# Sliding windows of an image batch: splitting every third store in the last loop, and copying on VectorE instead of ScalarE

## The chip, the core and the metric

The kernel runs on one core of a Trainium2 chip. The metric is the device time of one execution in microseconds. Before the change the median of three runs is 194.26 us (194.17 to 194.33).

## The reference: what is computed

The input `x` has 16 images of 64 channels, 64 x 64, in fp32. Every 8 x 8 window at a stride of 4 is copied out, so there are 15 x 15 windows and each element of the input goes to up to four of them. Nothing is calculated.

```python
batch, c, h, w = x.shape                 # 16, 64, 64, 64; window_size 8, stride 4
...
for i in range(n_h):                     # 15
    for j in range(n_w):                 # 15
        result[:, i, j] = x[:, :, 4*i : 4*i + 8, 4*j : 4*j + 8].copy()
```

The output is `[16, 15, 15, 64, 8, 8]`: 59 MB, from an input of 16.8 MB.

## The kernel before

**Layout.** A partition holds one image, one half of the channels (`CH` = 2, so 32 channels each) and one quarter of the rows (`HQ` = 4, so 16 rows each): 16 x 2 x 4 = 128 partitions. The whole input stays in SBUF as `L`, `[128, 32 channels, 16 rows, 64 columns]`. It is loaded in four chunks of channels with four DMAs each, issued in turn by SP and ACT; the first two chunks are the first half of a partition's channels.

**Windows.** The kernel works through 60 steps `(j, s)`: `j` is the column of the window (0 to 14) and `s` the place of its first row in a partition's quarter (0 to 3). One step makes, on all partitions at once, the windows of one column and of four rows of windows. `window(j, s, half)` gathers 32 channels x 8 x 8 elements per partition into the buffer `G`, and stores them from there with one indirect DMA, issued by POOL (GpSimd). A partition's piece of the output is one run of 8 KB; the row of the output that it goes to comes from an index tile. For `s` = 3 the window reaches into the next quarter: four rows are copied from the own partition (L103) and four are shuffled in from the next partition (L104), both on DVE (VectorE), and the last quarter of each image, which has no such window, is dropped by an index out of bounds. This is called a *last* window below (`idx_last`, `idx_hlast`). For `s` = 0, 1, 2 there is one copy (L101), on ACT (ScalarE).

**Wholes and halves.** With `half` = None a step is one *whole*: 32 channels, 2048 elements and 8 KB per partition, 1 MB in all (three quarters of it for a last window). With `half` = 0 or 1 it covers 16 of the channels: 1024 elements, 4 KB per partition. Halves use the output seen with rows of 4 KB (`o_h`, `idx_h`), wholes the one with rows of 8 KB (`o_v`, `idx`).

**Buffers.** `G` has 18 units, each for a half; a whole takes two. They are used in turn, so a copy waits until the store that last read its unit has finished. The stores are declared free of dependences among each other. Each uses one of eight semaphores, so a store waits for the eighth before it: at most eight are in flight.

**Order.** `order` goes over `j`, and within it over `s`. The first twelve steps store their first half early (L123), because only the first two chunks of the input must have landed for that. Then come six rounds of two second halves of those steps and two wholes of the following steps (L127). The last loop (L133) stores the remaining 36 steps, `j` from 6 to 14, as wholes. The framework schedules the instructions on each engine; in the trace POOL issues the first three last halves before the others, and otherwise follows the program.

Of the kernel before, what the change touches and what calls it, by code (L numbers as in the profile page):

```python
# [1 line left out]

# [4 lines left out]


@with_exitstack  # L10
def kernel(
    ctx: ExitStack,
    tc: tile.TileContext,
    x: bass.AP,
    window_size: int,
    stride: int,
    out: bass.AP,
):
    nc = tc.nc
    P = nc.NUM_PARTITIONS  # L20

    B, C, H, W = x.shape
    Bo, NH, NW, Co, WSo, WSo2 = out.shape
    WS = int(window_size)
    ST = int(stride)
    assert Bo == B and Co == C and WSo == WS and WSo2 == WS

    f32 = mybir.dt.float32
    i32 = mybir.dt.int32
    ALU = mybir.AluOpType  # L30
    HQ = 4
    CH = P // (B * HQ)
    CL = C // CH
    RB = H // HQ
    NSLOT = RB // ST
    NWIN = NH * NW
    CFREE = CL * WS * WS
    assert HQ == 4 and CH == 2 and WS == 2 * ST

    lpool = ctx.enter_context(tc.tile_pool(name="lpool", bufs=1))  # L40
    ipool = ctx.enter_context(tc.tile_pool(name="ipool", bufs=1))
    gpool = ctx.enter_context(tc.tile_pool(name="gpool", bufs=1))


    L = lpool.tile([P, CL, RB, W], f32)
    x_v = x.rearrange("b (ch cl) (hq r) w -> hq (b ch) cl (r w)", ch=CH, hq=HQ)
    NCH = 4
    cw = CL // NCH
    for k in range(NCH):
        for q in range(HQ):  # L50
            (nc.sync, nc.scalar)[q % 2].dma_start(
                out=L[q::HQ, k * cw : (k + 1) * cw, :, :],
                in_=x_v[q, :, k * cw : (k + 1) * cw, :],
            )


    def itile(name):
        return ipool.tile([P, 1], i32, name=name)

    pi, tb, tq, tc_, idx, idx_last = (itile(n) for n in ("pi", "tb", "tq", "tc", "idx", "idx_last"))  # L60
    nc.gpsimd.iota(pi[:, :], pattern=[[0, 1]], base=0, channel_multiplier=1)  # L61
    nc.vector.tensor_scalar(out=tb[:, :], in0=pi[:, :], scalar1=3, scalar2=None, op0=ALU.logical_shift_right)  # L62
    nc.vector.tensor_scalar(out=tc_[:, :], in0=pi[:, :], scalar1=2, scalar2=1, op0=ALU.logical_shift_right, op1=ALU.bitwise_and)  # L63
    nc.vector.tensor_scalar(out=tq[:, :], in0=pi[:, :], scalar1=HQ - 1, scalar2=None, op0=ALU.bitwise_and)  # L64
    nc.vector.tensor_scalar(out=tb[:, :], in0=tb[:, :], scalar1=float(NWIN * CH), scalar2=None, op0=ALU.mult)  # L65
    nc.vector.tensor_tensor(out=tb[:, :], in0=tb[:, :], in1=tc_[:, :], op=ALU.add)  # L66
    nc.vector.tensor_scalar(out=tc_[:, :], in0=tq[:, :], scalar1=float(NSLOT * NW * CH), scalar2=None, op0=ALU.mult)  # L67
    nc.vector.tensor_tensor(out=idx[:, :], in0=tb[:, :], in1=tc_[:, :], op=ALU.add)  # L68

    nc.vector.tensor_scalar(out=tq[:, :], in0=tq[:, :], scalar1=float(HQ - 1), scalar2=float(2 * B * NWIN * CH), op0=ALU.is_equal, op1=ALU.mult)  # L70
    nc.vector.tensor_tensor(out=idx_last[:, :], in0=idx[:, :], in1=tq[:, :], op=ALU.add)  # L71


    HCL = CL // 2
    idx_h, idx_hlast = itile("idx_h"), itile("idx_hlast")
    for d, e in ((idx_h, idx), (idx_hlast, idx_last)):
        nc.vector.tensor_scalar(out=d[:, :], in0=e[:, :], scalar1=2.0, scalar2=None, op0=ALU.mult)  # L77
    o_v = out.rearrange("b i j (ch cl) r w -> (b i j ch) (cl r w)", ch=CH)
    o_h = out.rearrange("b i j (ch cl) r w -> (b i j ch) (cl r w)", ch=2 * CH)
    nxt = [min(p + 1, 31) for p in range(32)]  # L80


    UNITS = 18
    G = gpool.tile([P, UNITS * HCL, WS, WS], f32, name="G")
    at = 0

    def window(j, s, half):
        nonlocal at
        cols = slice(j * ST, j * ST + WS)
        last = s == NSLOT - 1  # L90
        if half is None:
            n, c0 = 2, 0
            at += at % 2
        else:
            n, c0 = 1, half * HCL
        u = at % UNITS
        at += n
        cs = slice(c0, c0 + n * HCL)
        g = G[:, u * HCL : (u + n) * HCL, :, :]
        if not last:  # L100
            nc.scalar.copy(out=g, in_=L[:, cs, s * ST : s * ST + WS, cols])  # L101
        else:
            nc.vector.tensor_copy(out=g[:, :, 0:ST, :], in_=L[:, cs, s * ST : RB, cols])  # L103
            nc.vector.stream_shuffle(out=g[:, :, ST:WS, :], in_=L[:, cs, 0:ST, cols], mask=nxt)  # L104
        if half is None:
            o, ix = o_v, (idx_last if last else idx)
        else:
            o, ix = o_h, (idx_hlast if last else idx_h)
        st = nc.gpsimd.indirect_dma_start(  # L109
            out=o,  # L110
            out_offset=bass.IndirectOffsetOnAxis(ap=ix[:, 0:1], axis=0),
            in_=g.rearrange("p c r w -> p (c r w)"),
            in_offset=None,
            element_offset=(s * NW + j) * CH * CFREE + (half or 0) * HCL * WS * WS,
            bounds_check=B * NWIN * CH * (1 if half is None else 2) - 1,
            oob_is_err=False,
        )
        tc.declare_no_dep(st.ins, group="stores", reason="each store writes rows of its own")
        tc.add_to_no_dep_group("stores", st.ins)

    order = [(j, s) for j in range(NW) for s in range(NSLOT)]
    EARLY = 12
    for j, s in order[:EARLY]:  # L123
        window(j, s, 0)
    late = list(order[:EARLY])
    rest = list(order[EARLY:])
    while late:  # L127
        for w in late[:2]:
            window(*w, 1)
        for w in rest[:2]:  # L130
            window(*w, None)
        late, rest = late[2:], rest[2:]
    for w in rest:  # L133
        window(*w, None)


# [1 line left out]
_INS = ['x', 'window_size', 'stride']  # L138
_OUTS = [((16, 15, 15, 64, 8, 8), 'float32')]

_NUMBERS = {'window_size': 8, 'stride': 4}


# [26 lines left out]
```

## Time and profile before

| what | value |
|---|---|
| median of three runs | 194.26 us |
| the profiled execution: its time, and its span from first to last instruction | 194.17 us, 192.4 us |
| DVE, ACT, POOL busy | 30.4, 86.2, 70.3 us |
| HBM read, and stored by the POOL queue | 16.78 MB, 58.99 MB |
| stores: wholes, last wholes, halves, last halves | 36, 12, 18, 6 |
| one POOL issue of a store | 0.97 us |
| a whole copied on ACT; a half | 1.90 us; 1.04 us |
| half of a whole last window copied on DVE; shuffled | 0.69 us; 1.28 us |
| store, from issue to landing (whole; half) | 18.2 us; 13.6 us |
| last POOL issue; end of DMA traffic | 170.6 us; about 188.6 us |

Busy time is the time in which an engine executes; waiting and issuing of plain DMAs are not counted. "DMA share" is the mean busy share of the core's 16 DMA engines; it can come out slightly over 1, because consecutive packets overlap by a few ns. GB/s counts all that those engines moved, both ways.

### The profile page before, as it was taken

Reading aid. Unit: us, or ns where it says so; the run is one execution under the profiler, and the core shown is the slowest. Engines: PE = TensorE matmul, PEld = TensorE weight load, DVE = VectorE, ACT = ScalarE, POOL = GpSimd, SP = SyncE. Lnnn points to the kernel's source line nnn. Section 1 sums busy time; section 2 is a strip of 40 time slices with the busy share of each in tenths; the row PEclk is TensorE's granted clock in tenths of the full one; section 3 lists DMA queues with packets and bytes.
Section 4 is the critical chain, followed back from the end, with each engine's and each line's share of the span. In section 5 each row is a group of like instructions: output and inputs, shape, how many; then the busy total and the mean of one; then the engine's idle time right before and its main releaser. Section 6 shows DMA issues by size and latency. Waiting matters only on the chain.

```text
span 192.4 us, 478 instructions
## 1 busy us (share of the span) xinstructions
DVE 30.4 (16%) x65; ACT 86.2 (45%) x55; POOL 70.3 (37%) x77
## 2 busy tenths in 40 slices
DVE  2000050000232302303030122121121203030000
ACT  0000049500699875373747465646565655600000
POOL 0000027723367766456363253434343434440000
DMA  5999999999999999999999999999999999999960
GB/s 183 418 413 410 410 410 414 417 417 422 420 421 427 429 414 429 404 403 418 412 409 409 419 404 409 416 405 409 409 412 409 409 411 412 407 409 414 424 257 17
DMA packets 14724, 75.80 MB, mean 394 GB/s; under 512 B 1984, under 2 KB 1984, under 8 KB 8960
## 3 DMA queue, kind: packets, MB, share of 16 engines
q0 software_dynamic: 10368, 58.99, 75.3%
q1 hardware_dynamic: 2176, 8.39, 11.0%
q10 hardware_dynamic: 2176, 8.39, 10.8%
q14 instruction: 4, 0.03, 0.0%
HBM read 16.78 MB, written 62.91 MB: 414 GB/s over the span
## 4 chain that ended last, share of the span: by engine, by line
DMA 65%; issue 19%; ACT 3%; POOL 1%; POOLq 1%; PEldq 0%
DMA out_dram<-G,idx_last 38%; DMA out_dram<-G,idx 14%; DMA out_dram<-G,idx_h 8%; DMA out_dram<-G,idx_hlast 6%; ACT G L101 3%; POOL out_dram L109 1%; POOLq L165 1%; POOLq L109 0%; POOL pi L61 0%; PEldq L165 0%
## 5 line engine op out<-in xcount | busy, mean ns | idle before, releaser
L101 ACT COPY G<-L 128x2048 f32<-128x2048 f32 (+1 forms) x54 | 84.9, 1613 | 54.4 <-DMA out_dram<-G,idx 18.6
L109 POOL DMA_INDIRECT out_dram<-G,idx x36 | 34.8, 966 | 47.0 <-DMA out_dram<-G,idx 43.1
L103 DVE COPY G<-L 128x1024 f32<-128x1024 f32 (+1 forms) x18 | 11.1, 618 | 138.3 <-DMA out_dram<-G,idx 62.8
L109 POOL DMA_INDIRECT out_dram<-G,idx_h x18 | 17.4, 966 | 13.9 <-DMA out_dram<-G,idx_hlast 4.3
L104 DVE STREAM_SHUFFLE G<-L 128x1024 f32<-128x1024 f32 (+1 forms) x18 | 19.6, 1090 | 0.0
L109 POOL DMA_INDIRECT out_dram<-G,idx_hlast x6 | 5.9, 990 | 27.9 <-DVE G L104 26.4
L109 POOL DMA_INDIRECT out_dram<-G,idx_last x12 | 11.8, 986 | 11.7 <-DVE G L104 6.8
L101 ACT ACT_TABLE_LOAD x1 | 1.3, 1283 | 26.6 <-DMA L<-in_x_dram 26.6
L62 DVE TENSOR_SCALAR tb<-pi 128x1 int32<-128x1 int32 x1 | 0.2, 155 | 1.0 <-POOL pi L61 1.0
L61 POOL IOTA pi<- 128x1 int32 x1 | 0.1, 120 | 0.4 <-PEq L165 0.4
L104 DVE LOAD_MASK_SELECT G<-L x18 | 0.2, 14 | 0.0
L151 POOL MEMSET const-float32-0.0<- 128x1 f32 x1 | 0.1, 100 | 0.2 <-issue 0.2
L68 DVE CUSTOM_DVE_ANT_0 idx<-tb,tc 128x2 uint16<-128x2 uint16 x1 | 0.2, 160 | 0.0
L66 DVE CUSTOM_DVE_ANT_0 tb<-tb,tc 128x2 uint16<-128x2 uint16 x1 | 0.2, 159 | 0.0
L67 DVE TENSOR_SCALAR tc<-tq 128x1 int32<-128x1 int32 x1 | 0.2, 154 | 0.0
L77 DVE TENSOR_SCALAR idx_hlast<-idx_last 128x1 int32<-128x1 int32 x1 | 0.2, 154 | 0.0
L77 DVE TENSOR_SCALAR idx_h<-idx 128x1 int32<-128x1 int32 x1 | 0.2, 154 | 0.0
L71 DVE CUSTOM_DVE_ANT_0 idx_last<-idx,tq 128x2 uint16<-128x2 uint16 x1 | 0.2, 153 | 0.0
L65 DVE TENSOR_SCALAR tb<-tb 128x1 int32<-128x1 int32 x1 | 0.2, 152 | 0.0
L70 DVE TENSOR_SCALAR tq<-tq 128x1 int32<-128x1 int32 x1 | 0.1, 148 | 0.0
L64 DVE TENSOR_SCALAR tq<-pi 128x1 int32<-128x1 int32 x1 | 0.1, 145 | 0.0
L63 DVE TENSOR_SCALAR tc<-pi 128x1 int32<-128x1 int32 x1 | 0.1, 144 | 0.0
(3 smaller groups left out, 0.3 us busy)
## 6 DMA issues: line engine op xcount, KB each, us to landing
L<-in_x_dram ACTq DMA_DIRECT2D x8, 1024.0 KB, 21.1
L<-in_x_dram SPq DMA_DIRECT2D x8, 1024.0 KB, 19.8
out_dram<-G,idx POOLq DMA_INDIRECT x36, 18.2
out_dram<-G,idx_h POOLq DMA_INDIRECT x18, 13.6
out_dram<-G,idx_last POOLq DMA_INDIRECT x12, 18.3
out_dram<-G,idx_hlast POOLq DMA_INDIRECT x6, 13.1
```

Source lines behind the costliest of these rows:

```text
L62: nc.vector.tensor_scalar(out=tb[:, :], in0=pi[:, :], scalar1=3, scalar2=None, op0=ALU.logical_shift_right)
L65: nc.vector.tensor_scalar(out=tb[:, :], in0=tb[:, :], scalar1=float(NWIN * CH), scalar2=None, op0=ALU.mult)
L66: nc.vector.tensor_tensor(out=tb[:, :], in0=tb[:, :], in1=tc_[:, :], op=ALU.add)
L67: nc.vector.tensor_scalar(out=tc_[:, :], in0=tq[:, :], scalar1=float(NSLOT * NW * CH), scalar2=None, op0=ALU.mult)
L68: nc.vector.tensor_tensor(out=idx[:, :], in0=tb[:, :], in1=tc_[:, :], op=ALU.add)
L71: nc.vector.tensor_tensor(out=idx_last[:, :], in0=idx[:, :], in1=tq[:, :], op=ALU.add)
L77: nc.vector.tensor_scalar(out=d[:, :], in0=e[:, :], scalar1=2.0, scalar2=None, op0=ALU.mult)
L101: nc.scalar.copy(out=g, in_=L[:, cs, s * ST : s * ST + WS, cols])
L103: nc.vector.tensor_copy(out=g[:, :, 0:ST, :], in_=L[:, cs, s * ST : RB, cols])
L104: nc.vector.stream_shuffle(out=g[:, :, ST:WS, :], in_=L[:, cs, 0:ST, cols], mask=nxt)
L109: st = nc.gpsimd.indirect_dma_start(out=o, out_offset=bass.IndirectOffsetOnAxis(ap=ix[:, 0:1], axis=0), in_=g.rearrange("p c r w -> p (c r ...
L165: with _tile.TileContext(nc) as tc:
```

## The change

Two things are changed. The copy of a window with `s` = 0, 1, 2 is done by VectorE instead of ScalarE, in all stages, so that all gathering stands in one engine's queue and ScalarE only issues loads. And the last loop goes in groups of three steps: the first is stored as two halves, the next two as wholes. The 36 steps of this loop thus make 24 stores of halves and 24 of wholes instead of 36 of wholes, and the kernel has 84 stores instead of 72. The first two loops keep their order. Bytes, layouts, buffers and indices stay as they are.

```diff
         if not last:
-            nc.scalar.copy(out=g, in_=L[:, cs, s * ST : s * ST + WS, cols])
+            nc.vector.tensor_copy(out=g, in_=L[:, cs, s * ST : s * ST + WS, cols])
         else:
...
-    for w in rest:
-        window(*w, None)
+    while rest:
+        window(*rest[0], 0)
+        window(*rest[0], 1)
+        for w in rest[1:3]:
+            window(*w, None)
+        rest = rest[3:]
```

## The prediction

> **What bounds the kernel now.** I read the page first, then the busy time by stretch, the groups by shape, the timeline around the two engines that the change touches, and at last the trace's own records of DMA packets and of semaphore increments. The page says that the sixteen DMA engines are full from the second slice to the thirty-eighth, while no compute engine is above 45%:
>
> ```profile
> DVE 30.4 (16%) x65; ACT 86.2 (45%) x55; POOL 70.3 (37%) x77
> ...
> DMA  5999999999999999999999999999999999999960
> GB/s 183 418 413 410 410 410 414 417 417 422 420 421 427 429 414 429 404 403 418 412 409 409 419 404 409 416 405 409 409 412 409 409 411 412 407 409 414 424 257 17
> ```
>
> So the end is bytes over rate: 16.8 MB read and 59.0 MB stored. A copy, an issue or a wait counts only if it empties the DMA queues or changes the rate. The stretches (span us, their length, then DVE, ACT and POOL busy, clock, DMA share, GB/s) show three rates:
>
> ```profile
> 40.00:50.00 10.00, 0.20 (x1) 0.25 (x1) 2.90 (x3) 1.00 1.03 420
> 59.00:74.00 15.00, 2.95 (x6) 13.06 (x11) 10.03 (x11) 1.00 1.02 425
> 74.00:80.00 6.00, 1.83 (x4) 2.84 (x2) 2.90 (x3) 1.00 1.01 414
> 80.00:96.00 16.00, 3.27 (x6) 8.88 (x5) 8.43 (x9) 1.00 1.02 409
> 110.00:125.00 15.00, 3.72 (x6) 8.96 (x5) 6.47 (x7) 1.00 1.01 408
> 125.00:140.00 15.00, 3.21 (x6) 8.12 (x5) 5.85 (x7) 1.00 1.01 410
> 140.00:155.00 15.00, 2.50 (x4) 9.49 (x5) 6.03 (x7) 1.00 1.01 410
> 155.00:170.00 15.00, 3.79 (x6) 7.59 (x4) 5.80 (x6) 1.00 1.01 409
> 170.00:183.00 13.00, 0.00 (x0) 0.00 (x0) 0.97 (x1) 1.00 1.01 416
> 184.60:188.00 3.40, 0.00 (x0) 0.00 (x0) 0.00 (x0) 1.00 0.51 214
> ```
>
> Up to 97 us the engines move halves and wholes mixed (the last half is issued at 82.7 and lands about 14 us later), after that wholes alone. The tempting reading is "mixed runs at 425, wholes at 409, so mix throughout". The third and fourth lines speak against it: from 74 to 96 the stores are still the same mix, two halves and two wholes in turn, and the rate is already (6 x 414 + 16 x 409)/22 = 410.4. The packet records say the same. Until 73.5 us a 4 KB packet takes 159 ns and an 8 KB one 309 ns, nearly without exception; from 74 us on the means are about 164 and 321 for both sizes, mixed or not. Whatever slows packets by 4% begins inside the mixed stage.
>
> The last line is the second thing to see: for 3.4 us at the end half of the engines work alone. Each store makes sixteen semaphore increments, one as each engine finishes. The gap between the eighth and the ninth is 0.01 us until 77 us, then grows: 0.08 at 84, 0.82 at 94, 1.32 at 101 (0.73 us per 10 us), and from there more slowly, 1.49 at 106 to 3.48 at 179 (0.28 per 10 us). Eight engines run ahead, and the other eight set the end.
>
> **The change, part by part.** The last loop holds 36 windows (j from 6 to 14), 27 of 1.0486 MB and 9 of 0.7864 MB (a quarter of the rows of a last window is dropped): 35.4 MB, in 12 groups of three. The change splits the first window of each group.
>
> *Bytes and rate.* The bytes stay. Now this stage runs at 409.2 (mean of the four 15 us lines): 86.5 us. In the new mix the nearest row by time and state is 74 to 96, at 410.4, which already holds the cost of smaller packets and of more stores: 86.2 us, so **-0.3 us**. For the other ends: the full-speed mix at 425 gives 83.3, or -3.2; and from the packets alone, at full speed 16 packets of 4 KB at 155.3 ns start to start against 8 of 8 KB at 305.7, plus 6 ns for one more semaphore write, is +45 ns for each of 12 splits, or +0.5 us. I take -0.3 because that stretch has both the mix and the slow packets; I see nothing in the diff that removes what made them slow.
>
> *The gap between the engines.* If it grows by 0.73 per 10 us in a mix and 0.28 with wholes, 73 us (101 to 174) add up to 3.3 us of gap. A gap of s costs s x (1 - 214/409) = 0.48 s, since half the engines still work in it: 0 to +1.6 us. I take the middle, **+0.8**, since the steep stretch is also the one in which the gap arose, and may not keep its slope.
>
> *Twelve more stores on POOL.* An issue takes 0.97 us and 0.30 until the next: 1.27. A group of three windows takes the DMA 2.95 MB / 409 = 7.2 us; POOL then needs 4 x 1.27 = 5.1 in place of 3.8. Each store waits for the eighth before it, so eight are in flight: now eight wholes, then six window-equivalents, about 14 us of transfer. POOL's wait of 1.5 us or so at each store (44.6 us in all, for the eighth store back) shrinks, and this cover hides the rest: **0**. Without it each store would cost 1.27 us. The Trainium skill, page "DMA: Bandwidth & Descriptors", section "Anatomy of one DMA", gives a fixed cost of about 2.0 us per DMA, which would make an estimated 24 us of twelve stores if they ran one after another; here landings of queued halves follow each other every 1.23 us, so that rule does not price this case.
>
> *The copies from ACT to DVE.* Lines by shape:
>
> ```profile
> L101 ACT COPY G<-L 128x2048 f32<-128x2048 f32 x36 | 68.0, 1898 | 40.6 <-DMA out_dram<-G,idx 18.6 <-DMA out_dram<-G,idx_last 10.6 <-DVE G L104 8.0
> ...
> L104 DVE STREAM_SHUFFLE G<-L 128x1024 f32<-128x1024 f32 x12 | 15.3, 1279 | 0.0
> L103 DVE COPY G<-L 128x1024 f32<-128x1024 f32 x12 | 8.3, 694 | 81.1 <-DMA out_dram<-G,idx 62.8 <-DMA out_dram<-G,idx_h 10.2 <-ACT G L101 8.1
> ```
>
> DVE copies 512 elements in 0.42 us undisturbed and 1024 in 0.69; at 0.27 per 512 more, 2048 take an estimated 1.23 us (2.5 at worst, at the shuffle's pace). A group then costs DVE 1.6 us for the split window and 2.8 for two wholes with their share of last ones, 4.4 of 7.2 us (7.2 at the worst pace). Now all copies stand in one queue, so a copy that waits for its buffer holds up all later ones, and behind them POOL's stores. But the 18 half-buffers hold three groups, twelve stores, and eight are in flight: four stores, some 7 us, lie between a free buffer and its issue. Today it is one store, 2.5 us, against an ACT copy of 1.9. **0**.
>
> *The start.* The twelve first halves take DVE 9 x 0.69 + 3 x 1.13 = 9.6 us from 26.0 on, faster than POOL issues them (15 us), under loads that fill the DMA until 49.6. From 49.8 the second halves come 0.69 us apart instead of 1.04, with four or five stores still in flight. ACT's table load of 1.3 us goes, hidden. **0**.
>
> Sum: -0.3 + 0.8 = +0.5 us. The profiled run took 194.17 (span 192.39 and 1.78 around it), the median is 194.26: so 194.8.
>
> **The rivals.** *Faster: the slow packets vanish.* If they come from a relation between the engines' places in their stores that wholes on end keep up, and the new order breaks it, the last stage runs at 425 (-3.2 us), and with the gap gone a further 0.48 x 2.9 = -1.4: 191.1 without and 189.7 with the second. For it: 15 us at 425 in just this mix. Against: 22 us at 410 in the same mix. The 416 of 170 to 183, when no engine computes, says that quiet helps little.
>
> *Slower: DVE copies keep POOL from writing its descriptors.* The trace has one clear meeting:
>
> ```profile
> 60.65 0.43 DVE L103 COPY G<-L 128x512 f32<-128x512 f32 x1 [5.50 <-DMA out_dram<-G,idx_h]
> 60.70 1.21 POOL L109 DMA_INDIRECT out_dram<-G,idx_last  x1 [0.30 <-DMA out_dram<-G,idx_h]
> ```
>
> The issue took 1.21 instead of 0.97 under 0.38 us of copy; at 74.60 a copy of 512 took 0.69 behind a running issue instead of 0.43. So they exclude each other in part, and the copies on DVE, 18 now, would be 84. At +0.24 per store a POOL group is 4 x 1.51 = 6.0 us, below 7.2. At full exclusion it is 5.1 plus 3.4 of copying, 8.5. The last-loop issues begin at 88.4; 12 x 8.5 and 3 us for the last transfer end at 193.4 instead of 188.6, which is +4.8: 199. It decides from (188.6 - 3 - 88.4)/12 = 8.1 us per group, since the last issue is now at 170.5 and may slip. The Trainium skill, page "SBUF — State Buffer", section on the two sides of SBUF, states that an fp32 copy on DVE within SBUF locks GpSimd out for the whole instruction, so that descriptors starve: taken whole, that is the 199. The measured 0.24 says that the lock costs less than the overlap, and eight queued stores cover it.
>
> *No change in order or effect.* The program's order need not be the loop's (three last halves go out first today); the same bytes in another order, at the same 409 and the same gap, give 194.3.
>
> **How the numbers follow.** Forecast, rate about 410 with a gap that grows by anything from nothing to the full slope (193.9 to 196.0): 0.53, its lower part being "no change". Slow packets gone, wholly or partly (189.7 to 193.8): 0.34. POOL or DVE bound (above 196, up to 199): 0.13. A measurement of this kernel can tell about 0.2% from no change, 0.4 us: 193.9 to 194.65. That gives faster 0.34, same 0.18, slower 0.48. Signs are mixed, so the range runs into both rivals: 190.6 to 197.5; the forecast's own is 193.9 to 196.0.
>
> **What would show it.** Right: 409 to 411 GB/s from 80 to 170 us, 8 KB packets near 321 ns, a gap of 4 to 6 us between the engines at the end, DVE at about 100 us busy with copies of 1.2 us, ACT with none, POOL issues of 0.97 to 1.3 us. Wrong: rates above 415 after 80 us (first rival); DMA shares below 0.97 before 180 us, with POOL issues of 2 us (second); or a slow-down of packets that begins much earlier or later than 74 us, since I count on it staying where it is without knowing its cause.

## The result, and the profile after

The changed kernel takes 196.81 us (median of four runs, 196.75 to 196.88) against 194.30 for the kernel before: 2.5 us slower, a ratio of 1.0129 (95% interval 1.0112 to 1.0147). The sign of the forecast was right and its size was not: 0.5 us were forecast. The profiled execution took 196.88 us, with a span of 195.1.

The page of the changed kernel, its busy times, DMA rows and packet counts:

```profile
DVE 87.4 (45%) x137; POOL 99.9 (51%) x89
...
DMA  5999999999999999999999999999999999999940
GB/s 187 419 407 413 409 411 415 421 420 418 421 418 426 427 414 434 410 407 408 409 401 406 407 396 406 407 396 408 404 395 409 395 407 398 403 399 403 403 205 0
DMA packets 16452, 75.80 MB, mean 389 GB/s; under 512 B 2272, under 2 KB 2272, under 8 KB 12128
```

The DMA engines are as full as before, to the last slices, and they move the same 75.80 MB. So nothing starves; the engines move the bytes more slowly. The stretches of the changed kernel (span us, length, DVE and POOL busy, clock, DMA share, GB/s) show from where on:

```profile
59.00:74.00 15.00, 11.95 (x17) 12.26 (x10) 1.00 1.02 425
80.00:96.00 16.00, 10.14 (x16) 12.48 (x11) 1.00 1.02 410
96.00:110.00 14.00, 7.47 (x10) 8.94 (x8) 1.00 1.01 404
110.00:125.00 15.00, 9.24 (x15) 9.57 (x9) 1.00 1.01 402
125.00:140.00 15.00, 8.08 (x11) 9.07 (x8) 1.00 1.01 402
140.00:155.00 15.00, 9.23 (x15) 9.65 (x9) 1.00 1.02 402
155.00:170.00 15.00, 8.15 (x11) 9.01 (x8) 1.00 1.02 403
```

Up to 96 us, where both kernels move the same stores, the rates agree with those of before (425, then 409). From 96 on, where the stores differ, 414 and then 409 GB/s have become 404 and then 402. Of the kernel before, the row from 96 to 110 us is this one:

```profile
96.00:110.00 14.00, 1.97 (x4) 8.10 (x5) 6.07 (x7) 1.00 1.02 414
```

Three terms make up most of the difference, each read from the records of both traces. The 35.4 MB of the last loop take 86.5 us at 409 and 88.0 at 402.3: +1.5. The gap between the eighth and the ninth engine at the end is 4.3 us in place of 3.4, which at 0.48 us for each us of gap is +0.4. And POOL's program closes with a DRAIN instruction, which begins right after the last issue and is still running at the last landing (188.62 us before, 190.85 now); it ends 3.48 us after that landing instead of 2.99: +0.5. Together that is +2.4, of 2.5 by the medians and of 2.7 between the two profiled runs.

### The profile page after: what moved, and what is told of

Read it like the earlier page. It is cut to its first block, busy times and chain, and to the rows that moved or that the text cites. A ratio compares the mean times of both kernels' runs of the same rounds, so it can differ in the third digit from the quotient of the medians.

```text
span 195.1 us, 526 instructions
## 1 busy us (share of the span) xinstructions
DVE 87.4 (45%) x137; POOL 99.9 (51%) x89
## 2 busy tenths in 40 slices
DMA packets 16452, 75.80 MB, mean 389 GB/s; under 512 B 2272, under 2 KB 2272, under 8 KB 12128
## 4 chain that ended last, share of the span: by engine, by line
DMA 70%; issue 19%; POOL 1%; POOLq 1%; PEldq 0%
DMA out_dram<-G,idx 27%; DMA out_dram<-G,idx_last 21%; DMA out_dram<-G,idx_h 18%; DMA out_dram<-G,idx_hlast 4%; POOL out_dram L109 1%; POOLq L169 1%; POOLq L109 0%; POOL pi L61 0%; PEldq L169 0%
## 5 line engine op out<-in xcount | busy, mean ns | idle before, releaser
L101 DVE COPY G<-L 128x1024 f32<-128x1024 f32 (+1 forms) x63 | 57.4, 936 | 69.2 <-DMA L<-in_x_dram 39.1
L109 POOL DMA_INDIRECT out_dram<-G,idx_h x36 | 40.5, 1124 | 43.0 <-DVE G L101 26.0
L109 POOL DMA_INDIRECT out_dram<-G,idx x27 | 32.5, 1205 | 20.0 <-DMA out_dram<-G,idx 12.4
L104 DVE STREAM_SHUFFLE G<-L 128x512 f32<-128x512 f32 (+1 forms) x21 | 20.0, 953 | 0.0
L103 DVE COPY G<-L 128x512 f32<-128x512 f32 (+1 forms) x21 | 11.8, 564 | 13.7 <-DMA out_dram<-G,idx 12.2
L109 POOL DMA_INDIRECT out_dram<-G,idx_hlast x12 | 15.0, 1247 | 5.9 <-issue 3.4
```

Of the source, the lines that this page charges most:

```text
L101: nc.vector.tensor_copy(out=g, in_=L[:, cs, s * ST : s * ST + WS, cols])
L109: st = nc.gpsimd.indirect_dma_start(out=o, out_offset=bass.IndirectOffsetOnAxis(ap=ix[:, 0:1], axis=0), in_=g.rearrange("p c r w -> p (c r ...
```

## The experiments

Two theories stood against each other: that the splitting costs (A), or that the copies on VectorE do (B). The first four kernels separate the two parts, double one, and test whether neighbouring halves are to blame.

**split_act: the new order, copies left on ScalarE.** The edit undoes one line of the change:

```diff
-            nc.vector.tensor_copy(out=g, in_=L[:, cs, s * ST : s * ST + WS, cols])
+            nc.scalar.copy(out=g, in_=L[:, cs, s * ST : s * ST + WS, cols])
```

> The changed order, with the copies left on ScalarE. Theory A (the splitting costs: smaller packets and more stores, and a lower rate in the last stage): all of the 2.5 us remains, 196.5 to 197.0, with 402 to 404 GB/s from 110 to 170 us. Theory B (the copies on VectorE cost, through slower POOL issues or a disturbed DMA): the time is that of before, 194.1 to 194.5, at 409 GB/s. Theory C (both): in between, 195.0 to 196.2.

Measured: 196.72 us against 194.28, ratio 1.0128 (1.0113 to 1.0144): 2.44 us, all of the loss to within 0.1. The last stage, with the columns DVE, ACT and POOL busy again:

```profile
96.00:110.00 14.00, 2.34 (x4) 8.08 (x7) 6.93 (x8) 1.00 1.01 408
110.00:125.00 15.00, 3.84 (x9) 8.60 (x6) 7.87 (x9) 1.00 1.01 401
125.00:140.00 15.00, 2.44 (x4) 8.64 (x7) 7.58 (x8) 1.00 1.01 403
155.00:170.00 15.00, 2.49 (x4) 8.59 (x7) 7.52 (x8) 1.00 1.02 403
```

The rate is that of the changed kernel, though VectorE is as idle as before and POOL is busy for half of the time.

**whole_dve: the order of before, copies on VectorE.** The edit is the other part of the change alone (the first hunk of the diff).

> The order of before, with the copies on VectorE. Theory A: the time of before, 194.1 to 194.5, though POOL issues stretch to 1.0 to 2.0 us as they do in the changed kernel. Theory B: 196.5 to 197.0, with 402 to 404 GB/s in the last stage. Theory C: 195.0 to 196.2.

Measured: 194.61 us against 194.28, ratio 1.0019 (1.001 to 1.0028). The last stage runs at the rate of before from 110 us on, and without its 414 from 96 to 110:

```profile
80.00:96.00 16.00, 9.64 (x11) 12.95 (x11) 1.00 1.02 411
96.00:110.00 14.00, 7.67 (x10) 10.23 (x9) 1.00 1.01 410
110.00:125.00 15.00, 9.18 (x9) 8.12 (x7) 1.00 1.01 409
155.00:170.00 15.00, 8.63 (x10) 7.45 (x6) 1.00 1.01 409
```

So this order is 0.3 us slower with the copies on VectorE, and the split one by 0.1 (196.81 against 196.72, with ranges that overlap). The 0.3 lies outside the span from first to last instruction: that span has a median of 192.5 us here and before, and the eleven runs took 2.1 to 2.2 us beyond it, where those of before took 1.7 to 1.8. In the profiled run one of the four 8 KB loads of instructions falls at 194.2 us, 1.9 us after the last instruction; before, all four fall within the span. That this load makes the 0.3 is not shown. The stage itself loses nothing by the copies, so theory A holds.

**twosplit_act: 24 splits in place of 12**, copies on ScalarE:

```diff
-    for w in rest:
-        window(*w, None)
+    while rest:
+        for w in rest[:2]:
+            window(*w, 0)
+            window(*w, 1)
+        window(*rest[2], None)
+        rest = rest[3:]
```

> Copies on ScalarE, and two of each three windows of the last loop split, 24 splits in place of 12. Theory A: twice the cost of 12 splits: if that is 2.2 us, 198.5 to 199.0; if it is only what the packets cost at full speed (0.045 us a split), 195.3. Theory B: no more than 0.5 us over before, since POOL has 5 issues of 1.27 us in a group of 7.2 us, 194.3 to 195.3.

Measured: 198.96 us, ratio 1.0242 (1.0228 to 1.0256). Twelve splits cost 2.44 us, 24 cost 4.68: 0.20 us each, both times. The rate falls by another 7:

```profile
110.00:125.00 15.00, 3.79 (x9) 8.69 (x8) 9.64 (x10) 1.00 1.02 396
125.00:140.00 15.00, 2.31 (x6) 9.12 (x8) 9.59 (x10) 1.00 1.02 394
155.00:170.00 15.00, 2.28 (x6) 9.67 (x8) 9.63 (x10) 1.00 1.02 395
```

**crossed_act: the same 12 splits, but not the two halves of a window one after the other**, copies on ScalarE:

```diff
-    for w in rest:
-        window(*w, None)
+    while rest:
+        for half in (0, 1):
+            window(*rest[0], half)
+            window(*rest[3], half)
+            for w in rest[1 + 3 * half : 3 + 3 * half]:
+                window(*w, None)
+        rest = rest[6:]
```

> Copies on ScalarE, the same 12 splits, but the two halves of a window no longer follow each other: two first halves of different windows, two wholes, their two second halves, two wholes. If halves cost because neighbouring 4 KB of the same 8 KB row are written one straight after the other, this returns to 194.0 to 194.8, the time of wholes; if halves cost by their size and number alone, it equals the kernel with 12 splits on ScalarE within 0.3 us.

Measured: 196.68 us, ratio 1.0123 (1.0107 to 1.0138), against 196.72 with neighbouring halves. What counts is the size and the number of stores, which these runs don't separate, and not which half follows which.

The packet and landing records then split the 0.20 us. A packet is one partition's run of 4 or 8 KB. Packet times are means over 100 to 175 us, and the drain runs from the last landing to the end of POOL's DRAIN:

| kernel | stores | 8 KB packet, ns | 4 KB packet, ns | gap at the end, us | last landing, us | drain after it, us |
|---|---|---|---|---|---|---|
| before | 72 | 321.9 | - | 3.4 | 188.62 | 2.99 |
| whole_dve | 72 | 322.5 | - | 3.5 | 188.57 | 2.99 |
| split_act | 84 | 325.3 | 166.7 | 4.5 | 190.65 | 3.48 |
| after | 84 | 324.9 | 167.6 | 4.3 | 190.85 | 3.48 |
| twosplit_act | 96 | 328.2 | 168.6 | 4.8 | 192.28 | 3.97 |

At full speed, from 52 to 74 us, every one of these kernels has 159 and 309 to 310. So of 0.20 us a split the drain has 0.04 and the packets' full-speed price 0.045, as the prediction worked it out; the remaining 0.11 is that in the slow phase the packets of *both* sizes take longer still, and that the engines drift further apart.

The second set asked what the slow phase hangs on, and whether fewer splits make a faster kernel. All of it has the copies on ScalarE.

**early8_act and early6_act: fewer steps split early** (`EARLY = 8`, `EARLY = 6` in place of 12).

> The kernel before with 8 steps split in place of 12 (stores 68 in place of 72). If a split costs what 12 and 24 more of them cost in the last loop, 0.20 us, the time falls by 0.8 to 193.5; if the early ones, which run mostly before the packets slow down, cost only their packets at full speed (0.045) and POOL's closing drain (0.041 per store), by 0.35 to 193.9. Rival: the early halves are needed to bridge the time from the last load to the first store of a second half; then the DMA share falls below 1 near 50 us and the time rises.

> The kernel before with 6 steps split (66 stores). Without a gap after the loads 193.1 to 193.8; with five halves landed by 49.2 us only one is left for the 2 to 3 us until the first later store, so a gap of 1 to 2 us is likely and the time is 193.5 to 195.5. The drain after the last landing is 66 x 0.0414 = 2.73 us.

Both forecasts failed: 196.35 us (ratio 1.0104, 1.0088 to 1.0119) and 198.82 (1.0233, 1.0219 to 1.0247). The stretches of early8_act:

```profile
50.00:52.00 2.00, 2.00 (x6) 2.00 (x3) 0.73 (x1) 1.00 1.01 414
52.00:55.00 3.00, 0.84 (x1) 3.00 (x2) 2.39 (x3) 1.00 0.80 324
59.00:74.00 15.00, 3.78 (x6) 12.92 (x9) 11.44 (x12) 1.00 1.01 397
```

The rival of that expectation is the second line: a share of 0.80 over 3 us, 0.6 us of empty queue between the last early half and the first late one. With six it is 0.22 over 2 us and 0.51 over 3, 3.0 us. That isn't all of the loss of 2.1 and 4.5. The third line is the rest: 397 GB/s where the kernel before has 425. The 8 KB packets take 318 ns from 56 to 58 us and 320 to 335 in the stretches of 2 us from there to 74; the slow phase begins with the empty queue, 20 us sooner.

**bys_act and jdown_act: the same stores in another order.** One takes the 48 later steps by `s` and then `j` with every fourth a last one, the other takes `j` downward.

> The kernel before with the 48 later windows in another order: by s and then by j, with every fourth a last one; sizes, numbers and copies unchanged. If the slow packets come from which addresses meet, the rate from 110 to 170 us leaves 409 GB/s by more than 3 either way, or the onset leaves 74 us; if they come with time or with how far the engines are apart, 408 to 411 GB/s and 194.0 to 194.6.

> The kernel before with the later windows from j = 14 down to 3; sizes, numbers and copies unchanged. If the onset of the slow packets at 74 us hangs on the addresses of j = 4 and up, they are slow from the first whole on, near 59 us; if it hangs on time or on the sequence of sizes, it stays at 74 to 80 us and the time at 194.0 to 194.6.

Measured: 194.25 (ratio 0.9997, 0.9988 to 1.0007) and 194.28 (1.0000, 0.9990 to 1.0009). In both, packets take 309 ns up to 72 us, lengthen in the stretch from 74 to 76 (8 KB means of 313 and 315) and are at 321 to 322 from 76 to 78; before, it is 312 and 319. So neither the rate nor the onset changed with the order of the windows.

**early16_act and nolast_act.** The first has `EARLY = 16`; the second leaves out the twelve last wholes, 9.4 MB of the output.

> The kernel before with 16 steps split in place of 12 (76 stores). If a split costs its packets at full speed and its share of the closing drain, 4 x 0.086 = 0.35 us more, 194.6; if each costs 0.20 us as in the last loop, 195.1. If the deeper queue at the end of the loads keeps the packets at 159 and 309 ns past 74 us, up to 1 us less than the first figure.

> The kernel before without the twelve last wholes (s = 3, j from 3 to 14), so 9.4 MB of the output are not stored. If the last windows, which drop a quarter of their rows, break the state in which packets take 159 and 309 ns, the rate stays at 424 or more from 59 us to the end and the gap between the two halves of the engines stays below 0.5 us: about 169 us. If not, packets slow down near 74 us as before: 171 to 172 us, with a gap of 2 to 3 us.

Measured: 195.15 us with 16 (ratio 1.0045, 1.0032 to 1.0059): 0.82 us for four splits, again 0.20 each. Without last wholes, in one run, 170.0 us, between the two forecasts, and the slow phase comes all the same:

```profile
59.00:74.00 15.00, 1.12 (x3) 15.00 (x12) 9.29 (x10) 1.00 1.02 424
74.00:80.00 6.00, 1.32 (x3) 4.11 (x3) 3.25 (x4) 1.00 1.01 417
80.00:96.00 16.00, 0.00 (x0) 11.67 (x7) 7.71 (x8) 1.00 1.02 411
110.00:125.00 15.00, 0.00 (x0) 10.83 (x7) 5.22 (x7) 1.00 1.01 410
```

The gap at its end is 2.8 us. So the slow phase doesn't need last wholes, with their dropped rows, and VectorE, which does nothing here after 80 us, doesn't keep it going. The six last halves, which drop rows too, remain; the last of them stands near the onset, and whether it has a part in it is not tested.

**early10_act and early9_act: the smallest count that still fills the queue.**

> The kernel before with 10 steps split in place of 12 (70 stores). At 49.5 us five halves should still be queued, 6.2 us of transfer, against the 3.6 us that ran out with eight: no gap, packets at 159 and 309 ns until 70 us or later, and two splits fewer at 0.20 us each: 193.9, faster than before by 0.2%. If the queue runs dry after all, packets are slow from then on and the time is 195 or more.

> With 9 steps split (69 stores), 4.9 us queued at the end of the loads, against 0.6 us that were missing with eight: 193.7 if it just suffices, 195 to 196 if not. A state that is lost by the gap itself predicts a step in time between the counts that run dry and those that don't, of about 2 us, not a slope.

Measured: 194.29 (ratio 0.9998, 0.9989 to 1.0007) and 195.22 (1.0044, 1.0030 to 1.0057). The queue ran dry in neither. But the slow phase came sooner, at about 70 us with ten and at 60 with nine, as the stretches of early9_act show:

```profile
52.00:55.00 3.00, 1.85 (x3) 3.00 (x2) 2.13 (x3) 1.00 1.02 418
55.00:58.00 3.00, 0.00 (x0) 3.00 (x3) 1.93 (x2) 1.00 1.05 438
59.00:74.00 15.00, 3.82 (x6) 12.06 (x9) 11.34 (x13) 1.00 1.02 405
```

So the 0.4 us that two splits fewer should save was lost again, and with it fell the theory that only an empty queue ends the fast phase early. No version of these beats the kernel before.

What stays open is what ends the fast phase. It ended at 53 to 57 us in the two kernels with an empty queue, at 60, 70, 72 and mostly 74, and at 78 to 80 with the copies on VectorE. The order of windows, the last wholes and a dry queue are each excluded as its only cause; the runs don't name it. Why packets of both sizes take still longer in the slow phase when more of the stores are halves is open too.

## Why the prediction was right or wrong

The measured 196.81 us lies 0.8 above the forecast's own range (193.9 to 196.0). Only the wide range, which reaches into the rivals, contains it, and the stretch that it falls in (above 196) was set aside for a kernel bound by POOL or VectorE, which did not happen: DMA shares stayed at 1.00 to 1.02 and POOL's issues near 1.2 us. That the sign came out right is luck in part: the rate term had the wrong sign, the drain was left out, and the gap alone carried the +0.5. Two other signs failed with the rate: 8 KB packets took 325 ns and not 321, and VectorE was busy for 87 us and not about 100.

**The rate, -0.3 forecast, +1.5 measured: the term that failed.** I priced the new mix by the row from 74 to 96 us, 410.4, and the wholes by the rows from 110 to 170, 409.2 (-0.24 us without rounding), because the first had "both the mix and the slow packets". It had only the beginning of the slow phase. In every kernel of this study with twelve early steps 80 to 96 reads 409 to 411, whatever comes later; the 4 KB packets average 163.2 to 165.3 ns there and 166.3 to 168.6 after 100 us. No row of the trace before shows halves that late, so it could not give the price. It held a hint: the row next to the mix, 96 to 110, was wholes at 414, and I left it out. Compared next to next, 409 against 414, the mix costs 1.2%, of 86.5 us +1.0, with the right sign. The hint is weak, though: the same two rows read 411 and 412 in jdown_act and 411 and 410 in whole_dve. The upper bound that I set from full-speed packets, +0.5, was no upper bound either: in the slow phase of the changed kernel packets of both sizes take 5% longer than at full speed (4 KB 167.6 ns against 159, 8 KB 324.9 against 309 to 310), while the 8 KB packets of before take 4% longer (321.9).

**Twelve more stores on POOL, 0 forecast, +0.5 measured.** Issue and transfer cover each other as I said; what I overlooked comes after everything else. POOL's closing drain ends 2.99 us after the last landing with 72 stores, 3.48 with 84, 3.97 with 96, 2.74 with 66 and 2.50 with 60: 0.041 us per store in each. It lies on the path that sets the end, and the trace of before showed the 2.99 us that I counted as fixed.

The Trainium skill, page "DMA: Bandwidth & Descriptors", section "Anatomy of one DMA", has a fixed cost of about 2.0 us per DMA. Measured end to end, one more store of a split costs 0.20 us here, with several in flight.

**The gap, +0.8 forecast, +0.4 measured.** The mechanism was there and the size was within the stated ends (0 to 1.6). It ended at 4.3 us, inside the forecast 4 to 6. Its slope did not stay at 0.73 us per 10 us: from 101 to 174 us the gap grew from 1.2 to 4.1, 0.40 per 10 us.

**The copies on VectorE, 0 forecast, 0.1 measured beside the splits.** With wholes alone it was 0.3, outside the span. The durations came out as estimated, 1.24 us for 2048 elements and 0.70 for 1024, and the four stores of slack covered the single queue. Groups of the changed kernel:

```profile
L109 POOL DMA_INDIRECT out_dram<-G,idx_h x36 | 40.5, 1124 | 43.0 <-DVE G L101 26.0 <-DMA out_dram<-G,idx_h 7.8 <-issue 7.3
L101 DVE COPY G<-L 128x2048 f32<-128x2048 f32 x27 | 33.4, 1244 | 25.3 <-DMA out_dram<-G,idx 22.1 <-DMA out_dram<-G,idx_last 3.1
L109 POOL DMA_INDIRECT out_dram<-G,idx x27 | 32.5, 1205 | 20.0 <-DMA out_dram<-G,idx 12.4 <-issue 3.7 <-DVE G L104 1.9
L101 DVE COPY G<-L 128x1024 f32<-128x1024 f32 x36 | 24.4, 704 | 43.9 <-DMA L<-in_x_dram 39.1 <-DMA out_dram<-G,idx_h 4.0 <-DMA out_dram<-G,idx_hlast 0.3
```

POOL's issues did stretch, from 0.97 to a mean of 1.12 to 1.29 us. The longest meeting in the changed kernel, first as VectorE's timeline shows it (start, length, and three copies in a row merged into one line), then as POOL's does:

```profile
59.58 3.10 DVE L101 COPY G<-L 128x2048 f32<-128x2048 f32 x3
```

```profile
60.19 2.00 POOL L109 DMA_INDIRECT out_dram<-G,idx_hlast  x1 [0.30 <-issue]
```

The issue takes twice its time and still ends before the copies do, so it is not shut out for all of them. Four issues of 1.2 and 0.30 us between make 6.0 us per group, as worked out with 0.24 per meeting, below the 8.1 from which this rival would have decided. The Trainium skill, page "SBUF — State Buffer", section on the two sides of SBUF, says that GpSimd cannot write descriptors while such a copy runs, and that the DMA engines then sit idle. The stretched issues agree with the first; the second is not seen here, at shares of 1.00 to 1.02.

**The other rivals.** The faster one is excluded: no split returned the packets to 159 and 309 ns in the last stage. That the order might not take effect didn't happen: 12,128 packets under 8 KB in place of 8,960 are 3,168 more, the 4 KB packets of 24 halves and 288 small completion writes.

## What to carry to other kernels

When the DMA queues are full, a change of store size is priced by the rate. The speed of the same packets drifts within a run, so the stretch that stands for the new mix must lie as far into the run's slow phase as the stage that is priced; if none does, a run of the mix has to give the price. Count what each DMA costs after the last byte has landed; that part of the end grows with the number of DMAs and nothing hides it. And a stretch that ran fast with some mix does not show that the mix made it fast: run the two parts of such a change one by one.

## What the runs showed of the hardware

- POOL's closing DRAIN ends 0.041 us per indirect store of the program after the last landing, from 60 stores (2.50 us) to 96 (3.97).
- The same packets have a fast phase, 159 ns for 4 KB and 309 for 8 KB with hardly an exception, and a slow one, 163 to 169 and 319 to 328 as means of a stage. Each run here began its stores in the first and went over to the second once, between 53 and 80 us, and stayed there, single stretches of 2 us apart, until half of the engines had finished.
- In the slow phase two sets of eight engines drift apart by 0.3 to 0.7 us per 10 us, to 2.8 to 4.8 us at the end; the eight that are left alone then run at 309 ns again.
- POOL's issue of a store and VectorE's copy of fp32 within SBUF hold each other up only in part: an issue of 0.97 us became 2.0 at the worst.
